# Down projection of a two-layer hybrid encoder: seven products of quarters for a pair of output blocks, with attention buffers in shared memory

## The chip, the cores and the metric

The kernel runs on one core of a Trainium2 chip. The metric is the device time of one execution in microseconds (us), the median of several runs. PE is TensorE, DVE VectorE, ACT ScalarE, POOL GpSimd and SP SyncE, which issues most DMAs.

## The reference

One inference step of an encoder with two layers (`DEPTH = 2`), for a prompt of 512 positions and a sample of 32 positions that share all weights; model width 1024, hidden width 4096. Each layer is

```
x = x + W_out(concat[A(h), B(h), C(h)]),  h = rms_norm(x, g_mix)
hf = rms_norm(x, g_ffn)
x = x + jnp.square(jax.nn.relu(hf @ w_up)) @ w_down
```

A, B and C are a spatial gate, a short convolution and a sparse attention whose keys an indexer picks (top k). The outputs are x after the second layer and the new cache rows. The change concerns the last line, the product with `w_down` (4096 x 1024).

## The kernel before, in words

x stays in SBUF feature-major: 8 blocks of 128 features by 544 positions, as two tiles, one for each half of the positions (`xs[0]` with 256 and `xs[1]` with 288 columns). A float32 product is made of three float32r products: each operand is split into a part `hi` (a cast on ACT) and a part `lo` (a subtraction on DVE), and hi·hi, lo·hi and hi·lo are summed in PSUM (`mm3`, L225 to L227).

Weights come in through `load_w` (L205): SP issues a DMA of 512 KB into one of two `raw` buffers, ACT casts its 1024 columns to `hi` (L216), DVE (for a few loads POOL) makes `lo` (L217), and both go into a ring of 3072 columns, so three such loads are on hand ahead of PE.

The feed-forward of a layer is cut into four chunks c of 1024 hidden features. A chunk has an **up phase**, 8 blocks f of 128 features, each 8 k-blocks x 3 matmuls for each half (L225 to L227, the moving operand `h0hi` to `h1lo`), after which ACT takes relu (L957), DVE squares (L958) and `split` writes `hi` and `lo` of the activations (L221 and L222: `a0hi` to `a1lo`). Its **down phase** is 8 output blocks m, each 24 matmuls for each half with the activations as moving operand; `add_to_x` (L908) on DVE adds the sum in PSUM to x. So a down phase is 8 x 2 x 24 = 384 matmuls, half of them 256 and half 288 columns wide.

At the end of layer 0 the last three output blocks are taken together, all of the first half and then all of the second, so that the norm of the first half (`norm`, L252 to L258: a matmul with ones, rsqrt with a Newton step, then 8 blocks scaled and split) lies beside the second half's matmuls. At the end of layer 1 the transposed results (`results`, L273 to L277) of one half of the positions lie in the same way beside the matmuls of the other.

The order on each engine is fixed when the program is built: a scheduler takes what is ready, by a priority that favours copies out of PSUM (`EVAC`) and then weight loads (`PREP`). At run time every engine works through its list in that order.

Of the kernel before, what the change touches and what calls it, by code (L numbers as in the profile page):

```python
# [7 lines left out]
F32 = mybir.dt.float32  # L8
F32R = mybir.dt.float32r
# [6 lines left out]
D = 1024  # L16
# [4 lines left out]
HALF = (256, 288)  # L21
EPS = 1e-6
# [3 lines left out]
# column groups of w_in  # L26
# [12 lines left out]
class Shift:  # L39
    """Shifts the scheduling priority of what is traced inside."""  # L40
# [12 lines left out]
def kernel(  # L53
# [13 lines left out]
    rawp = ctx.enter_context(tc.tile_pool(name="rawp", bufs=2))  # L67
# [48 lines left out]
    busy = keep([128, 512], "qrs")  # L116
# [5 lines left out]
    spare = keep([128, 2, D], "a1hi"), keep([128, D], "a0hi")  # L122
    xin += [spare[0][:, 0], spare[0][:, 1], spare[1]]
    # per-feature vectors as columns: g_mix, g_ffn, conv_w, state_conv
# [20 lines left out]
    xs = [keep([128, 8, n], f"x{i}") for i, n in enumerate(HALF)]  # L145
# [11 lines left out]
    junk = keep([128, 2, D], "a0lo")  # L157
# [61 lines left out]

    def split(hi, lo, src):  # L220
# [43 lines left out]
    def results(b, g, tag):  # L264
        """A block's output, half of its features, back to token-major."""
# [15 lines left out]
    def prepare(l):  # L281
# [42 lines left out]
    def search_constants():  # L324
# [3 lines left out]
        # for the threshold search: prefix sums, the copies' total, steps  # L328
# [15 lines left out]
    for l in range(depth):  # L344
# [20 lines left out]
        def tok_gemm(b, pieces, n, aside=True):  # L365
            """Token-major product of a block; aside: the sample's rows by themselves, in float32."""
# [678 lines left out]
```

## Time and profile before

| | |
|---|---|
| median of 3 runs (lowest to highest) | 1400.22 us (1398.63 to 1400.79) |
| span of the profiled execution | 1403.4 us |
| busy: PE, DVE, ACT, POOL | 1353.1, 840.0, 615.9, 115.3 us |
| mean granted TensorE clock | 0.982 of full speed |

The profile is of one execution on the chip. A row of a group names line, engine, operation, output and inputs and shapes; a row of a timeline starts with the start and the length in us; in square brackets stands the idle time of that engine just before and what ended it. The length of a matmul is longer than its distance to the next, since matmuls are pipelined. Times below are of this execution.

### The profile page before, as it was taken

The page shows a single profiled execution, that of the slowest core. Times are in us where ns is not written, and L with a number is a line of the kernel's source. Part 1 is how long each engine was busy: PE and PEld are TensorE (multiplying, and loading weights), DVE is VectorE, ACT ScalarE, POOL GpSimd, SP SyncE. Part 2 cuts the span into 40 slices and gives each one's busy share as a digit, 9 for nine tenths or more (in the row PEclk, how much of TensorE's full clock was granted, in tenths as well). Part 3 has the DMA queues.
Part 4 walks back from the last instruction along what each step waited for, and adds up shares of the span by engine and source line. Part 5 has one row for each costly group of instructions (what it writes and reads, how often), then busy time and mean ns, then how long its engine had stood idle before and what let it go on. Part 6 is the DMA issues. An engine that isn't in the chain of part 4 may idle for free. (4 is left out here: it accounts for less than half of the span.)

```text
span 1403.4 us, 25751 instructions
## 1 busy us (share of the span) xinstructions
PE 1353.1 (96%) x10430; PEld 1265.8 (90%) x10430; DVE 840.0 (60%) x2103; ACT 615.9 (44%) x1212; POOL 115.3 (8%) x125
## 2 busy tenths in 40 slices
PE   7998999998999999999989899999899999999998
PEld 5877886898999999999987789779799999999998
DVE  6999987468434334334489999865853343443442
ACT  5746996335314224223246489842542231331321
POOL 4414200010000000000042120000200000000000
PEclk8999999999999999999988999999999999999999
DMA  7124221323233332333212222222233332233322
GB/s 185 33 71 106 68 64 48 94 68 89 81 88 91 91 84 84 89 91 91 64 49 62 58 81 77 76 61 61 61 95 88 91 91 86 82 90 91 91 81 74
DMA packets 183566, 113.00 MB, mean 81 GB/s; under 512 B 7028, under 2 KB 180616, under 8 KB 183448
## 3 DMA queue, kind: packets, MB, share of 16 engines
q1 hardware_dynamic: 180808, 106.35, 26.2%
q0 software_dynamic: 2640, 5.01, 1.8%
q8 instruction: 82, 1.34, 0.4%
q14 instruction: 36, 0.29, 0.1%
HBM read 106.67 MB, written 4.67 MB: 79 GB/s over the span
## 5 line engine op out<-in xcount | busy, mean ns | idle before, releaser
L216 ACT CAST hi<-raw 128x1024 fp32r<-128x1024 f32 (+1 forms) x188 | 194.1, 1032 | 404.6 <-PE psm L226 389.1
L217 DVE TENSOR_TENSOR lo<-raw,hi 128x1024 fp32r<-128x1024 f32 (+1 forms) x163 | 197.5, 1212 | 174.9 <-ACT hi L216 174.2
L908 DVE TENSOR_TENSOR x<-x,psm 128x256 f32<-128x256 f32 (+1 forms) x192 | 83.7, 437 | 232.4 <-PE psm L227 232.0
L226 PE MATMUL psm<-h1lo,hi 128*128 128x288 f32 x640 | 190.4, 298 | 0.9 <-DVE h1lo L222 0.9
L227 PE MATMUL psm<-a1hi,lo 128*128 128x288 f32 x640 | 190.0, 297 | 0.0
L226 PE MATMUL psm<-a1lo,hi 128*128 128x288 f32 x640 | 189.9, 297 | 0.0
L225 PE MATMUL psm<-a1hi,hi 128*128 128x288 f32 x640 | 189.8, 297 | 0.0
L225 PE MATMUL psm<-h1hi,hi 128*128 128x288 f32 x640 | 188.7, 296 | 1.1 <-ACT h1hi L221 1.1
L227 PE MATMUL psm<-h1hi,lo 128*128 128x288 f32 x640 | 189.1, 296 | 0.0
L226 PE MATMUL psm<-h0lo,hi 128*128 128x256 f32 x640 | 181.9, 285 | 6.2 <-DVE h0lo L222 6.2
L225 PE MATMUL psm<-a0hi,hi 128*128 128x256 f32 x640 | 183.0, 286 | 0.0
L226 PE MATMUL psm<-a0lo,hi 128*128 128x256 f32 x640 | 182.0, 284 | 0.0
L227 PE MATMUL psm<-a0hi,lo 128*128 128x256 f32 x640 | 182.0, 284 | 0.0
L225 PE MATMUL psm<-h0hi,hi 128*128 128x256 f32 x640 | 181.4, 284 | 0.0
L227 PE MATMUL psm<-h0hi,lo 128*128 128x256 f32 x640 | 180.0, 282 | 0.0
L226 PEld LDWEIGHTS psm<-h0lo,hi 128*128 128x128 f32 x640 | 120.4, 188 | 8.6 <-DVE h0lo L222 7.1
L225 PEld LDWEIGHTS psm<-h1hi,hi 128*128 128x128 f32 x640 | 120.1, 188 | 2.7 <-ACT h1hi L221 1.5
L225 PEld LDWEIGHTS psm<-a0hi,hi 128*128 128x128 f32 x640 | 121.6, 190 | 0.5 <-issue 0.5
L226 PEld LDWEIGHTS psm<-h1lo,hi 128*128 128x128 f32 x640 | 120.3, 188 | 1.8 <-DVE h1lo L222 1.3
L226 PEld LDWEIGHTS psm<-a0lo,hi 128*128 128x128 f32 x640 | 121.2, 189 | 0.6 <-issue 0.5
L225 PEld LDWEIGHTS psm<-h0hi,hi 128*128 128x128 f32 x640 | 120.6, 189 | 1.2 <-issue 0.9
L227 PEld LDWEIGHTS psm<-a0hi,lo 128*128 128x128 f32 x640 | 121.6, 190 | 0.0
(318 smaller groups left out, 2841.1 us busy)
## 6 DMA issues: line engine op xcount, KB each, us to landing
raw<-in_w_up_dram SPq DMA_DIRECT2D x64, 512.0 KB, 4.1
raw<-in_w_down_dram SPq DMA_DIRECT2D x64, 512.0 KB, 3.9
raw<-in_w_in_dram SPq DMA_DIRECT2D x36, 512.0 KB, 3.9
raw<-in_w_out_dram SPq DMA_DIRECT2D x8, 512.0 KB, 3.8
raw<-in_w_out_dram SPq DMA_DIRECT2D x32, 128.0 KB, 3.0
raw<-in_w_in_dram SPq DMA_DIRECT2D x8, 296.0 KB, 6.1
q<-in_cache_k_dram SPq DMA_DIRECT2D x4, 512.0 KB, 4.3
h1lo<-in_cache_v_dram SPq DMA_DIRECT2D x2, 1024.0 KB, 7.1
```

The source lines that it names most:

```text
L216: nc.scalar.copy(hi, raw)
L217: (eng or nc.vector).tensor_tensor(lo, raw, hi.bitcast(F32), op=ALU.subtract)
L225: nc.tensor.matmul(out, lhsT=st[0], rhs=mv[0], start=first, stop=False)
L226: nc.tensor.matmul(out, lhsT=st[0], rhs=mv[1], start=False, stop=False)
L227: nc.tensor.matmul(out, lhsT=st[1], rhs=mv[0], start=False, stop=last)
L908: nc.vector.tensor_tensor(xs[h][:, m, :], xs[h][:, m, :], p[:, :HALF[h]], op=ALU.add)
```

## The change

For a chunk, the weights of a **pair** of output blocks (m1, m2) are four quarters: L11 and L21 are the first 512 hidden features for m1 and for m2, L12 and L22 the other 512. The activations are four quarters too: R11 and R12 the first four f-blocks for positions 0 to 271 (A) and 272 to 543 (B), R21 and R22 the other four. Sums of quarters are made on DVE: T1 = R12 - R11, T2 = R22 - T1, T3 = R22 - R12, T4 = R21 - T2 once a chunk, and S1 = L21 + L22, S2 = S1 - L11, L12 - S2 and L11 - L21 for each pair. Seven products of 4 k-blocks x 3 matmuls, 272 columns wide, take the place of the eight that four quarter products of each side need. They are summed in three PSUM tiles (tags l, d, o), and after each of the seven DVE adds a tile to one quarter of x. The weights are split after the sums, in pieces of 512 columns (`split_w`), so the ring holds six pieces. x is one tile, `raw` has three buffers, the scratch memory of POOL's DMAs is set to 8192 bytes, and the activations R11, R21, R22 and T1 lie in `ahi`/`alo`; T2, T3 and T4 lie in six buffers `e0` to `e5` that the attention uses for keys, values, scores and queries. Both norms at the end of layer 0, and all five blocks of results of the last 512 features of layer 1, now come after the last product.

```diff
-    rawp = ctx.enter_context(tc.tile_pool(name="rawp", bufs=2))
+    rawp = ctx.enter_context(tc.tile_pool(name="rawp", bufs=3))
...
+    def split_w(src, a, c):
+        with prep:
+            if ring[2] + a * c > RING:
+                ring[2] = 0
+            hi, lo = (t[:, ring[2]:ring[2] + a * c].rearrange("p (k c) -> p k c", k=a) for t in ring[:2])
+            ring[2] += a * c
+            nc.scalar.copy(hi, src)
+            nc.vector.tensor_tensor(lo, src, hi.bitcast(F32), op=ALU.subtract)
+        return [(hi[:, k], lo[:, k]) for k in range(a)]
+    def sum_w(a, b, op):
+        with prep:
+            t = T(512, "tt").rearrange("p (k c) -> p k c", k=4)
+            nc.vector.tensor_tensor(t, a, b, op=op)
+        return t
...
+        kTp = keep([128, 2, NT], "e0")
+        Vp = keep([128, 4, 256], "e1")
+        works = keep([128, SK], "e2")
+        qTs = keep([128, 2, 2, 2, 128], "e3")
+        mixed = keep([128, 1024], "e4")
+        work3, qrs = mixed[:, :512], mixed[:, 512:].rearrange("p (u c) -> p u c", u=2)
+        kiTq = keep([128, NT + 256], "e5", F32R)
+        kiTp = kiTq[:, :NT]
...
-            act = [(keep([128, 8, n], f"a{h}hi", F32R), keep([128, 8, n], f"a{h}lo", F32R)) for h, n in enumerate(HALF)]
-            for fs in ((0, 1, 2), (3,), (4,), (5,), (6,), (7,)) if c == 0 else [(f,) for f in range(8)]:
...
+                for f in fs:
+                    k = f % 4
+                    if f < 4:
+                        put(R11, k, hidden[f][:, :EVEN])
+                        continue
+                    r1, r2 = hidden.pop(k), hidden.pop(f)
+                    t12, t34 = T(NT + NS, "pt"), T(NT + NS, "pt")
+                    A, B = slice(0, EVEN), slice(EVEN, 2 * EVEN)
+                    sub = lambda o, a, b: nc.vector.tensor_tensor(o, a, b, op=ALU.subtract)
+                    sub(t12[:, A], r1[:, B], r1[:, A])
+                    split(*(t[:, R21:R22 + 1, k, :] for t in first4), r2.rearrange("p (a n) -> p a n", a=2))
+                    put(T1, k, t12[:, A])
+                    sub(t12[:, B], r2[:, B], t12[:, A])
+                    put(T2, k, t12[:, B])
+                    sub(t34[:, A], r2[:, B], r1[:, B])
+                    sub(t34[:, B], r2[:, A], t12[:, B])
+                    put(T3, k, t34[:, A])
+                    put(T4, k, t34[:, B])
...
-            last, end = c == 3 and l + 1 < depth, c == 3 and l + 1 == depth
-            for ms in ((0,), (1,), (2,), (3,), (4,), (5, 6, 7)) if c == 3 else [(m,) for m in range(8)]:
-                ws = [load_w(w_down[l, c * 1024:c * 1024 + 1024, m * 128:m * 128 + 128], 8, 128) for m in ms]
-                for h in (1, 0) if end else (0, 1):
-                    for m, w in zip(ms, ws):
-                        p = fm_gemm(h, act, w)
-                        add_to_x(h, m, p)
...
+            def product(p, w, o, first=True):
+                for k in range(4):
+                    st, mv = w[k], [t[:, k, :] for t in parts_of[o]]
+                    for a, b in ((0, 0), (0, 1), (1, 0)):
+                        nc.tensor.matmul(p[:, :EVEN], lhsT=st[a], rhs=mv[b], start=first and (k, a, b) == (0, 0, 0),
+                                         stop=(k, a) == (3, 1), skip_group_check=True)
+            def quarters(i):
+                rows = lambda q: w_down[l, c * 1024 + q * 512:c * 1024 + q * 512 + 512, i * 256:i * 256 + 256]
+                ra, rb = load_raw(rows(0), 4, 256), load_raw(rows(1), 4, 256)
+                l11, l21, l12, l22 = ra[:, :, :128], ra[:, :, 128:], rb[:, :, :128], rb[:, :, 128:]
+                part = lambda v: split_w(v, 4, 128)
+                yield part(l11)
+                s1 = sum_w(l21, l22, ALU.add)
+                yield part(s1)
+                s2 = sum_w(s1, l11, ALU.subtract)
+                yield part(s2)
+                yield part(sum_w(l12, s2, ALU.subtract))
+                yield part(l12)
+                yield part(sum_w(l11, l21, ALU.subtract))
+                yield part(l22)
...
+            for i in range(4):
+                m1, m2 = 2 * i, 2 * i + 1
+                w = quarters(i)
+                pa, pb, pd = psum("l"), psum("o"), psum("d")
+                product(pa, next(w), R11)
+                add(m1, 0, pa)
+                product(pd, next(w), T1)
+                add(m2, 1, pd)
+                finish()
+                product(pa, next(w), T2, first=False)
+                add(m1, 1, pa)
+                product(pd, next(w), R22, first=False)
+                add(m1, 1, pd)
+                product(pb, next(w), R21)
+                add(m1, 0, pb)
+                product(pa, next(w), T3, first=False)
+                add(m2, 1, pa)
+                def end_pair(pa=pa, w=w, m1=m1, m2=m2):
+                    product(pa, next(w), T4, first=False)
+                    add(m2, 0, pa)
+                    squares_of(m1)
+                late.append(end_pair)
+                if end and i == 2:
+                    for b, tag in enumerate("mxmxm"):
                         results(b, 0, tag)
+            finish()
+            if last:
+                for h in range(2):
+                    hn.append(norm(h, o_gm + 8 * (l + 1)))
+            if end:
+                for b, tag in enumerate("mxmxm"):
+                    results(b, 1, tag)
...
-    nc = _bacc.Bacc("TRN2", target_bir_lowering=False, num_devices=1)
+    nc = _bacc.Bacc("TRN2", target_bir_lowering=False, num_devices=1, dynamic_dma_scratch_size=8192)
```

How the instructions move on the engines is seen at three places.

DVE within a down phase (chunk 1 of layer 0), the preparation of weights (`lo`) and the additions to x. Before:

```order
764 L217 TENSOR_TENSOR lo<-raw_4755,hi 128x1024
765 L908 TENSOR_TENSOR x_8_105<-x_8_105,psm_4647 128x256
766 L908 TENSOR_TENSOR x_9_106<-x_9_106,psm_4673 128x288
767 L217 TENSOR_TENSOR lo<-raw_4811,hi 128x1024
768 L908 TENSOR_TENSOR x_8_105<-x_8_105,psm_4703 128x256
769 L908 TENSOR_TENSOR x_9_106<-x_9_106,psm_4729 128x288
```

Now, from the second addition of a pair's fourth product on (L244 are sums of weights, the tiles `t_` hold them, `ps` are PSUM tiles):

```order
951 L1030 TENSOR_TENSOR x_104<-x_104,psd_5755 128x272
952 L244 TENSOR_TENSOR t_5976<-raw_5876 128x512
953 L238 TENSOR_TENSOR lo<-t_5927,hi 128x512
954 L1030 TENSOR_TENSOR x_104<-x_104,pso_5754 128x272
955 L238 TENSOR_TENSOR lo<-t_5944,hi 128x512
956 L1030 TENSOR_TENSOR x_104<-x_104,psl_5753 128x272
957 L238 TENSOR_TENSOR lo<-raw_5878,hi 128x512
958 L1030 TENSOR_TENSOR x_104<-x_104,psl_5873 128x272
959 L238 TENSOR_TENSOR lo<-t_5976,hi 128x512
960 L244 TENSOR_TENSOR t_6015<-raw_5996,raw_5998 128x512
961 L1030 TENSOR_TENSOR x_104<-x_104,psd_5875 128x272
962 L238 TENSOR_TENSOR lo<-raw_5996,hi 128x512
```

Two splits of 1024 columns and four additions to a pair of blocks have become seven splits of 512, four sums of 512 and seven additions of 272 columns.

DVE at the turn from the up to the down phase of the same chunk, with the last block of activations (L958 and L1007 are the squares, L222 and L249 the `lo` of activations, L1016 the differences). Before:

```order
757 L958 TENSOR_TENSOR t_4552<-t_4552 128x256
758 L222 TENSOR_TENSOR a0lo_4072<-t_4552,a0hi_4071 128x256
759 L217 TENSOR_TENSOR lo<-raw_4699,hi 128x1024
760 L958 TENSOR_TENSOR t_4582<-t_4582 128x288
761 L908 TENSOR_TENSOR x_8_105<-x_8_105,psm_4591 128x256
762 L222 TENSOR_TENSOR a1lo_4074<-t_4582,a1hi_4073 128x288
763 L908 TENSOR_TENSOR x_9_106<-x_9_106,psm_4617 128x288
764 L217 TENSOR_TENSOR lo<-raw_4755,hi 128x1024
```

Now (`ahi` and `alo` of two 272-column pieces are R21 and R22, `e_931` is T2 and `e_933` T3):

```order
919 L1007 TENSOR_TENSOR t_5577<-t_5577 128x288
920 L244 TENSOR_TENSOR t_5856<-raw_5756 128x512
921 L1030 TENSOR_TENSOR x_104<-x_104,psl_5648 128x272
922 L238 TENSOR_TENSOR lo<-raw_5756,hi 128x512
923 L1030 TENSOR_TENSOR x_104<-x_104,psd_5650 128x272
924 L249 TENSOR_TENSOR alo_5097<-t_5577,ahi_5096 128x2x272
925 L238 TENSOR_TENSOR lo<-t_5775,hi 128x512
926 L1016 TENSOR_TENSOR t_5632<-t_5577,t_5632 128x272
927 L1016 TENSOR_TENSOR t_5633<-t_5577,t_5516 128x272
928 L1016 TENSOR_TENSOR t_5633<-t_5577,t_5632 128x272
929 L249 TENSOR_TENSOR e_932_5099<-t_5632,e_931_5098 128x272
930 L249 TENSOR_TENSOR e_934_5101<-t_5633,e_933_5100 128x272
```

The differences and splits of the last block, and with them T2, stand behind the additions of the first two products.

PE at the end of layer 0. Before, from the last down matmuls into the products of layer 1's indexer (`h0hi` is the first half's norm):

```order
4799 L225 MATMUL psm_7992<-a1hi_6965,hi 128x288
4800 L226 MATMUL psm_7992<-a1lo_6966,hi 128x288
4801 L227 MATMUL psm_7992<-a1hi_6965,lo 128x288
4802 L225 MATMUL psm_8093<-hi,h0hi_7900 128x296
4803 L226 MATMUL psm_8093<-lo,h0hi_7900 128x296
4804 L227 MATMUL psm_8093<-hi,h0lo_7901 128x296
```

Now (`psx` is the sum of squares for the norms, L279):

```order
4603 L1037 MATMUL psl_8083<-e_1103_7166,hi 128x272
4604 L1037 MATMUL psl_8083<-e_1104_7167,hi 128x272
4605 L1037 MATMUL psl_8083<-e_1103_7166,lo 128x272
4606 L279 MATMUL psx_8243<-work_1161_7873,ones 128x256
4607 L279 MATMUL psx_8286<-work_1163_7877,ones 128x288
4608 L252 MATMUL psm_8365<-hi,h0hi_8252 128x296
4609 L253 MATMUL psm_8365<-lo,h0hi_8252 128x296
4610 L252 MATMUL psm_8407<-hi,h0hi_8252 128x296
```

The sums for both norms stand between the last product and the indexer, where before the indexer followed the last product at once.

## Rows read from the trace of the kernel before

**Rows 1.** The page: span, and busy time with share and instructions of each engine.
```profile
span 1403.4 us, 25751 instructions
PE 1353.1 (96%) x10430; PEld 1265.8 (90%) x10430; DVE 840.0 (60%) x2103; ACT 615.9 (44%) x1212; POOL 115.3 (8%) x125
```

**Rows 2.** Windows: length; busy us (count) of PE, PEld, DVE, ACT, POOL; PEclk; DMA; GB/s.
```profile
369.60:418.20 48.60, 48.60 (x386) 48.60 (x385) 17.09 (x25) 9.14 (x10) 0.00 (x0) 1.00 0.30 87
418.20:466.60 48.40, 48.40 (x386) 48.40 (x385) 22.23 (x39) 19.23 (x38) 0.00 (x0) 1.00 0.31 88
338.00:700.00 362.00, 362.00 (x2871) 362.00 (x2870) 152.63 (x255) 110.41 (x193) 0.00 (x0) 1.00 0.31 88
709.90:738.10 28.20, 22.68 (x140) 21.04 (x142) 22.56 (x61) 11.93 (x32) 12.71 (x15) 0.84 0.14 40
```

**Rows 3.** Timeline, down projection in layer 0: start, length, engine, line, operation.
```profile
411.99 0.29 PE L227 MATMUL psm<-a1hi,lo 128*128 128x288 f32 x1
412.12 0.28 PE L225 MATMUL psm<-a0hi,hi 128*128 128x256 f32 x1
412.24 0.29 PE L226 MATMUL psm<-a0lo,hi 128*128 128x256 f32 x1
412.32 0.45 DVE L908 TENSOR_TENSOR x<-x,psm 128x288 f32<-128x288 f32 x1 [2.78 <-PE psm L227]
```

**Rows 4.** Groups by shape, whole span: busy us, mean ns, idle before, releaser.
```profile
L217 DVE TENSOR_TENSOR lo<-raw,hi 128x1024 fp32r<-128x1024 f32 x158 | 193.5, 1224 | 172.2 <-ACT hi L216 171.6 <-DMA raw<-in_w_out_dram 0.5
L908 DVE TENSOR_TENSOR x<-x,psm 128x288 f32<-128x288 f32 x96 | 43.5, 453 | 166.7 <-PE psm L227 166.7
L908 DVE TENSOR_TENSOR x<-x,psm 128x256 f32<-128x256 f32 x96 | 40.2, 420 | 65.8 <-PE psm L227 65.3
L222 DVE TENSOR_TENSOR a0lo<-t,a0hi 128x256 fp32r<-128x256 f32 x72 | 30.6, 425 | 29.2 <-ACT a0hi L221 29.2
L216 ACT CAST hi<-raw 128x592 fp32r<-128x592 f32 x8 | 5.5, 685 | 4.3 <-DMA raw<-in_w_in_dram 3.0 <-PE psm L226 1.3
```

**Rows 5.** Timeline of DVE in an up projection, instructions that follow without a wait.
```profile
425.47 1.23 DVE L217 TENSOR_TENSOR lo<-raw,hi 128x1024 fp32r<-128x1024 f32 x1 [2.44 <-ACT hi L216]
426.61 0.45 DVE L958 TENSOR_TENSOR t<-t 128x288 f32<-128x288 f32 x1
427.56 0.46 DVE L222 TENSOR_TENSOR a1lo<-t,a1hi 128x288 fp32r<-128x288 f32 x1 [0.50 <-ACT a1hi L221]
427.94 0.42 DVE L958 TENSOR_TENSOR t<-t 128x256 f32<-128x256 f32 x1
```

**Rows 6.** Groups of DVE in the down projection at 369.6 to 418.2.
```profile
L217 DVE TENSOR_TENSOR lo<-raw,hi 128x1024 fp32r<-128x1024 f32 x8 | 9.8, 1226 | 5.8 <-ACT hi L216 5.8
```

**Rows 7.** Timeline at the end of layer 0.
```profile
713.30 0.41 PE L227 MATMUL psm<-hi,h0lo 128*128 128x296 f32 x1 [0.90 <-DVE h0lo L222]
716.03 1.33 PE L252 MATMUL psx<-work,ones 128*128 128x288 f32 x2 [2.19 <-DVE work L242]
721.60 0.45 PE L226 MATMUL psm<-lo,h0hi 128*128 128x296 f32 x1
721.84 0.45 PE L227 MATMUL psm<-hi,h0lo 128*128 128x296 f32 x1
...
722.40 0.30 PE L227 MATMUL psm<-hi,h0lo 128*128 128x296 f32 x1
...
726.44 1.19 DVE L222 TENSOR_TENSOR h1lo<-t,h1hi 128x288 fp32r<-128x288 f32 x3
```

**Rows 8.** DMA issues of the page: KB each, median us to landing.
```profile
raw<-in_w_down_dram SPq DMA_DIRECT2D x64, 512.0 KB, 3.9
out_dram<-t SPq DMA_DIRECT2D x8, 256.0 KB, 2.1
```

**Rows 9.** Timeline at the end of the program.
```profile
1397.70 0.28 PE L227 MATMUL psm<-a0hi,lo 128*128 128x256 f32 x1
1399.52 0.82 SPq L277 DMA_DIRECT2D out_dram<-t  x2
```

More of the change, by code (lines that the diff above doesn't have):

```diff
@@ L21 @@
 HALF = (256, 288)
+EVEN = (NT + NS) // 2
+QTR = 4 * EVEN
 EPS = 1e-6
@@ L121 @@
     xin = [Q([128, D]), Q([128, D])]
-    spare = keep([128, 2, D], "a1hi"), keep([128, D], "a0hi")
-    xin += [spare[0][:, 0], spare[0][:, 1], spare[1]]
+    spare = keep([128, 4 * QTR], "ahi")
+    xin += [spare[:, i * D:i * D + D] for i in range(3)]
     NV = 8 * depth * 2 + 6 * depth + 4 * depth
@@ L218, in load_w, with load_raw @@
         return [(hi[:, k], lo[:, k], raw[:, k]) for k in range(a)]
+    def load_raw(src, a, c):
+        with prep:
+            raw = rawp.tile([128, a, c], F32, tag="raw", name=nm("raw"))
+            nc.sync.dma_start(raw, src.rearrange("(k p) c -> p k c", p=128))
+        return raw
+    def split_w(src, a, c):
[8 more added lines that the diff above has]
+    def sum_w(a, b, op):
+        with prep:
+            t = T(512, "tt").rearrange("p (k c) -> p k c", k=4)
+            nc.vector.tensor_tensor(t, a, b, op=op)
+        return t
     def split(hi, lo, src):
@@ L570 @@
                     nc.vector.tensor_copy(wsel[:, :, a, :], pt[:, :64].rearrange("p (g t) -> p g t", g=2))
-                work = keep([128, SK], "works")
+                work = works
                 for c0, cn in ((0, 512), (512, 512), (1024, 32)):
@@ L944, with put @@
         hn = []
+        R11, R21, R22, T1, T2, T3, T4 = range(7)
         for c in range(4):
-            act = [(keep([128, 8, n], f"a{h}hi", F32R), keep([128, 8, n], f"a{h}lo", F32R)) for h, n in enumerate(HALF)]
-            for fs in ((0, 1, 2), (3,), (4,), (5,), (6,), (7,)) if c == 0 else [(f,) for f in range(8)]:
+            last, end = c == 3 and l + 1 < depth, c == 3 and l + 1 == depth
+            first4 = [keep([128, 4, 4, EVEN], tag, F32R) for tag in ("ahi", "alo")]
+            rest = [[keep([128, 4, EVEN], f"e{3 * i + j}", F32R) for i in range(2)] for j in range(3)]
+            parts_of = [[t[:, o] for t in first4] for o in range(4)] + rest
+            def put(o, k, src):
+                split(parts_of[o][0][:, k, :], parts_of[o][1][:, k, :], src)
+            hidden = {}
+            order = (0, 4, 1, 5, 2, 6, 3, 7)
+            groups = [order[:3]] + [(f,) for f in order[3:]] if c == 0 else [(f,) for f in order]
+            for fs in groups:
                 ws = []
@@ L950 @@
                     c0 = (c * 8 + f) * 128
-                    ws.append(load_w(w_up[l, :, c0:c0 + 128], 8, 128, nc.gpsimd if c == 0 and f < 3 else None))
+                    ws.append(load_w(w_up[l, :, c0:c0 + 128], 8, 128, nc.gpsimd if c == 0 and f in order[:3] else None))
+                    hidden[f] = T(NT + NS, "g")
                 for h, n in enumerate(HALF):
@@ L968, with finish, squares_of @@
+            late = []
+            def finish():
+                while late:
+                    late.pop()()
+            def squares_of(m0):
+                if last:
+                    for m in (m0, m0 + 1):
+                        for h in range(2):
                             add_square(h, m)
@@ L970 @@
                                 heat(h, m)
-                    if last and len(ms) == 3:
-                        hn.append(norm(h, o_gm + 8 * (l + 1)))
-                    if end and len(ms) == 3:
-                        for b, tag in ((0, "l"), (1, "x")) if h == 0 else ((2, "l"), (3, "x"), (4, "o")):
-                            results(b, 1, tag)
-                if end and ms == (4,):
-                    for b, tag in enumerate("lxold"):
-                        results(b, 0, tag)
+            for i in range(4):
[22 more added lines that the diff above has]
+                    for b, tag in enumerate("mxmxm"):
+                        results(b, 0, tag)
+            finish()
+            if last:
+                for h in range(2):
+                    hn.append(norm(h, o_gm + 8 * (l + 1)))
+            if end:
+                for b, tag in enumerate("mxmxm"):
+                    results(b, 1, tag)
         hs = hn
```

30 lines of the change are left out of this document (15 added, 15 removed).

## The prediction

> **What bounds the kernel now.** I read the page first: the span is 1403.4 us and PE is busy for 1353.1 of it, no other engine for more than 60% [rows 1]. The profiled execution is 3.2 us longer than the median of 1400.22, so I make the sum on 1403.4 and take 3.2 off at the end. Then the windows, because a mean over stages says nothing of one: in a down phase and in an up phase of the feed-forward PE is busy every microsecond, DVE 17.09 of 48.60 and 22.23 of 48.40, and the clock is at its upper level, 2.4 GHz [rows 2]. The reader is to see there that the feed-forward is paced by matmuls alone: 2871 of them fill 362.00 us, 126.1 ns each. Third, the timeline, for what one matmul costs: the next starts 0.13 us after one of 288 columns and 0.12 us after one of 256 [rows 3], though each is 0.28 or 0.29 us long. Distance counts, not length; it grows with the columns, and 272 lie in the middle, so I take the mean of 126.1 ns for them. Last, the groups by shape and DVE's timeline, for the new work.
>
> **The matmuls.** Eight down phases have 384 each, 3072. The change has 7 products x 12 x 4 pairs x 8 = 2688. 384 fewer at 126.1 ns: **-48.4 us**, all of it on the path. A pair goes from 96 x 0.1261 = 12.11 us to 84 x 0.1261 = 10.59, a product takes 1.51.
>
> **DVE in the down phase.** A pair needs 7 `lo` and 4 sums of 512 columns and 7 additions of 272. No row has these shapes. By length, 512 lie between 425 ns (256 columns) and 1224 ns (1024): 425 + 256/768 x 799 = 691; 272 between 420 and 453: 437 [rows 4]. But neighbours overlap: after the 1.23 us split the next instruction starts 1.14 us later, after one of 0.46 us 0.38 later [rows 5], so DVE is held some 0.085 us less: 0.605 and 0.35. A pair costs 11 x 0.605 + 7 x 0.35 = 9.1 us, against 10.59 of PE: 86%, where today it is 17.09 / 48.60 = 35% [rows 2]. ACT has 7 casts of under 0.685 us [rows 4], under 4.8 us. So the work lies beside the matmuls, but the cover is thin, and two things can lift it. First, the order of PE is fixed, and a product that goes on in a PSUM tile (S2·T2 on L11·R11) waits for the addition that reads it; one other product, 1.51 us, stands between, and an addition starts about 0.33 us after the last matmul of its sum [rows 3], 0.35 later it is done: 0.8 us to spare, one piece of preparation. Second, three `raw` buffers serve pairs that take two, so a pair's second load starts only when the sum L11 - L21 of the pair before is made, and takes 3.9 us [rows 8]; in the new order four products' additions stand between, some 4.5 us, and the sum that needs it would hold up DVE by little. I take 0.2 us a pair, 32 x 0.2 = **+6 us**; ends 0 and 0.7 a pair (+22), the latter a missed hand-over of one 512-column piece each time.
>
> **DVE in the up phase.** For two blocks f, four differences, one split of 544 and five of 272 columns replace four splits: 9 x 0.35 + 0.65 - 4 x 0.35 = 2.4 us, so a phase goes from 22.2 to about 32 us of 48.4 [rows 2]. Covered, nothing. In the first chunk of a layer it falls beside the norms: +0.5 each, **+1 us**.
>
> **The turn from up to down.** Today the last block's split is needed 24 matmuls later. Now T2, T3 and R21/R22 of the last k-block stand in DVE's list behind the additions of the first two products. From the last up matmul on: square, sum and addition end at about 2.2 us, `lo` and the second addition (its product ends at 3.0) at 3.7, then split of 544, `lo` and three differences, 0.65 + 0.6 + 1.05 = 2.3, so T2 is whole at about 6.4. PE has 45 matmuls, 5.7 us, that do not need it, and then a few that need only its `hi`. It waits for some 0.4: 8 x 0.4 = **+3 us**. Ends 0 and 2.5 (the whole DVE run uncovered), +20.
>
> **The end of layer 0.** Today the first half's norm runs beside 72 matmuls, and still the stretch from there to the end of the indexer's five blocks takes 28.20 us with PE busy 22.68 and a clock of 0.84 [rows 2]: PE waits for 0.90 and 2.19 us, and from the second wait on the distance of its matmuls is 0.24 us, the level of 1.2 GHz, for about 6 us, until 0.13 returns [rows 7]. Now nothing runs beside either norm: addition, squares, their sums, matmul, rsqrt, three steps, scaling and cast follow each other, ten steps of about 0.45 us, 4.5 us. Then 48 matmuls of 0.135, paced by 16 DVE steps of about 0.36 (three take 1.19 us [rows 7]), 6.5; then the ropes of two blocks before the second half is scaled, 3; then 72 matmuls, 9.7; and 3 us for a slow clock as today: 26.7, and 0.7 for the last product of the pair, which waits for the addition of the one before. That is a microsecond less than today, with a longer list of waits; I take **+2 us**, ends -3 and +12 (the low level for the whole stretch, 120 x 0.105).
>
> **The last pair and the tail.** The sums of weights take buffers from which results are being written out; a store needs 2.1 us to land [rows 8] and stands between: 1 to 2 us. At the end five result blocks remain after the last matmul instead of two; today the last store is issued 1.8 us after it [rows 9], now one more pair of transposes and copy, 1.1 us. Together **+3 us**, ends +1 and +6. What the norms of layer 0 share with the attention buffers is free by then: the attention of a layer ends before its output projection. The smaller scratch memory concerns POOL, 8% busy [rows 1], and nothing on the path.
>
> **Sum.** 1403.4 - 48.4 + 6 + 1 + 3 + 2 + 3 = 1370.0 us; less 3.2 it is **1367 us**.
>
> **The rivals.** *DVE sets the pace of the down phases.* If each instruction holds DVE for its whole length, a pair costs 11 x 0.691 + 7 x 0.437 = 10.7 us, more than PE's 10.59, and the first sum and cast of a pair (0.6 us) come on top: 11.3 a pair, a gain of 0.8 x 32 = 26 and with 12 us for the ends 1386 us. Against it stands the overlap in rows 5. [...] Chance 0.15.
>
> *Every `lo` waits for its cast: slower.* Today a `lo` in a down phase finds DVE idle for 5.8 / 8 = 0.73 us until ACT has cast [rows 6]. With seven a pair on a DVE that works through its list in order, 9.1 + 7 x 0.73 = 14.2 us, 2.1 more than 12.11: 32 x 2.1 = +67, with 12 for the ends 1479 us. It decides from (12.11 - 9.1)/7 = 0.43 us a `lo` on. Against it: a ring of six pieces lets a cast start five products ahead, and the order of DVE puts other work between a sum and its `lo`. Chance 0.06.
>
> *The ends lose their cover.* 2.5 us at each turn and 10 at the end of layer 0: 1367 + 17 + 8 = 1392 us. For it speaks that DVE is behind after an up phase; against it that PE's order puts other products ahead of T2. Chance 0.09.
>
> *It doesn't save what it counts.* If 272 columns go at the distance of 288, 0.1325, the products cost 2688 x 0.1325 = 356 us against 387, a gain of 31 in place of 48: 1384 us. Rows 3 show a distance that grows with columns. Chance 0.04.
>
> **How the numbers follow.** The forecast has 0.66 and spans 1350 (all of the 48 us, the ends as low as they go) to 1380. The range reaches to the two rivals at 1384 and 1386 and part of the way to 1392: 1350 to 1390. Only the second rival is slower; a measurement here tells 0.2%, 2.8 us, from no change. Faster 0.92, same 0.02, slower 0.06.
>
> **What would show it.** Right: in a window of a down phase PE busy all through, 336 matmuls in 42 to 44 us, DVE about 36 of it, distances of 0.126 us; at each turn a wait of under 1 us on `e3` or `e0`. Wrong: PE waiting for `lo` or for `x` in every pair (the first two rivals), DVE over 95% in that window, waits of 2 us at the turns, or the clock at 1.2 GHz for much longer than 6 us after layer 0.

## The result, and the profile after

The changed kernel takes **1362.27 us** (median of 5 runs, 1359.95 to 1367.17) against 1398.63 for the kernel before in the same comparison: ratio 0.9742, 95% interval 0.9718 to 0.9766, a gain of 36 us where 33 were forecast. The profiled execution is the longest of the five (1367.17; span 1365.4), so where its stages are compared below, a second profile of the same kernel stands beside it.

The page of after, the lines that answer to [rows 1]:

```profile
span 1365.4 us, 25930 instructions
PE 1308.2 (96%) x10046; PEld 1220.7 (89%) x10046; DVE 1079.1 (79%) x2679; ACT 709.8 (52%) x1436; POOL 111.9 (8%) x125
```

PE has 384 matmuls fewer and is as full as before; DVE has gone from 60 to 79%. The windows of after, columns as in [rows 2]: 27 products of the down phase of chunk 0 in layer 0, the whole down phase of chunk 1, the up phase of chunk 2, the end of layer 0.

```profile
368.01:409.05 41.04, 41.04 (x327) 40.96 (x326) 34.78 (x68) 18.18 (x30) 0.00 (x0) 1.00 0.32 95
459.27:503.05 43.78, 43.78 (x347) 43.57 (x346) 36.18 (x69) 18.18 (x30) 0.00 (x0) 1.00 0.34 98
503.18:550.51 47.33, 47.33 (x376) 47.33 (x375) 34.00 (x67) 22.16 (x46) 0.00 (x0) 1.00 0.29 88
684.50:712.00 27.50, 21.82 (x122) 20.51 (x121) 20.53 (x61) 9.57 (x27) 6.79 (x11) 0.81 0.13 39
```

The reader is to see PE busy in every microsecond of a down phase, with DVE at 36.18 of 43.78 (the window holds the 336 matmuls of the phase and a few of the next up phase). 27 products are 324 matmuls in 41.04 us, 126.7 ns each; the distance that was taken is 126.1. A chunk begins 91.25 us after the one before it (368.01, 459.27, 550.51, 641.77) where it was 97.0, so a chunk is worth 5.75 us and eight of them 46. That is 2.4 us less than the 48.4 of the prediction: all 720 matmuls of a chunk go at 126.7 ns, where the 768 of before went at 126.3. DVE's timeline in that phase, the lines that answer to [rows 5]:

```profile
472.37 0.68 DVE L238 TENSOR_TENSOR lo<-raw,hi 128x512 fp32r<-128x512 f32 x1
472.98 0.69 DVE L244 TENSOR_TENSOR t<-t,raw 128x512 f32<-128x512 f32 x1
473.58 0.43 DVE L1030 TENSOR_TENSOR x<-x,psl 128x272 f32<-128x272 f32 x1
473.93 0.69 DVE L238 TENSOR_TENSOR lo<-t,hi 128x512 fp32r<-128x512 f32 x1
```

Start to start it is 0.60 after 512 columns and 0.35 after 272, the two prices of the prediction (0.605, 0.35), and the lengths are 0.69 and 0.43 (0.691, 0.437). The groups of these shapes over the span, with the idle time that stands in front of them:

```profile
L238 DVE TENSOR_TENSOR lo<-t,hi 128x512 fp32r<-128x512 f32 x128 | 88.2, 689 | 14.1 <-ACT hi L237 11.1
L238 DVE TENSOR_TENSOR lo<-raw,hi 128x512 fp32r<-128x512 f32 x96 | 66.1, 689 | 9.0 <-ACT hi L237 5.0
L1037 PE MATMUL psl<-e,hi 128*128 128x272 f32 x768 | 151.9, 292 | 1.1 <-DVE x L1030 1.1
```

A `lo` waits for its cast for 16.1 us over 224 of them, 0.07 us each, where [rows 6] had 0.73. The last row holds the only wait of PE inside the seven products of the whole program: 1.1 us, in the last pair of layer 0. PE's timeline of the end of layer 0, rows with a wait in front alone (compare [rows 7]), and the wait that came new behind it:

```profile
684.03 0.48 PE L1037 MATMUL psl<-e,hi 128*128 128x272 f32 x2 [1.07 <-DVE x L1030]
687.21 0.70 PE L279 MATMUL psx<-work,ones 128*128 128x256 f32 x2 [1.44 <-DVE work L269]
688.90 0.75 PE L279 MATMUL psx<-work,ones 128*128 128x288 f32 x2 [0.99 <-DVE t L157]
690.78 0.62 PE L252 MATMUL psm<-hi,h0hi 128*128 128x296 f32 x1 [1.12 <-ACT h0hi L248]
702.47 0.41 PE L252 MATMUL psm<-hi,h1hi 128*128 128x296 f32 x1 [2.12 <-ACT h1hi L248]
...
724.74 0.37 PE L106 MATMUL psl<-idr,ks 128*128 128x128 f32 x1 [4.62 <-ACT t L582]
```

The span is 38.0 us shorter than that of before. Eight chunks give -46.0. From the last product of layer 0 (685.49) to the last matmul of the indexer (715.56) it is 30.1 us, before 27.6: +2.5. The last down phase and the tail together lose 1. The start, up to the first product of layer 0, is 1.6 shorter (368.0 for 369.6), which says nothing: in the ten profiles of the changed kernel and its variants it takes from 361.7 to 368.0 us. What is left is +6.0 between 715.56 and the first product of layer 1 (1038.62): 323.1 us where it was 317.0. The prediction had 0.5 us there (DVE beside the norms in the first chunk), and the experiments go after the rest.

### The profile page after: what moved, and what is told of

Read it like the earlier page. It is cut to its first block, busy times and chain, and to the rows that moved or that the text cites. A ratio compares the mean times of both kernels' runs of the same rounds, so it can differ in the third digit from the quotient of the medians.

```text
span 1365.4 us, 25930 instructions
## 1 busy us (share of the span) xinstructions
PE 1308.2 (96%) x10046; PEld 1220.7 (89%) x10046; DVE 1079.1 (79%) x2679; ACT 709.8 (52%) x1436; POOL 111.9 (8%) x125
## 4 chain that ended last, share of the span: by engine, by line
PE 82%; DVE 11%; issue 3%; ACT 2%; DMA 2%; POOL 0%; SPq 0%; ACTq 0%; DVEq 0%; POOLq 0%
PE psm L253 16%; PE psm L252 16%; PE psm L254 15%; PE psl L1037 14%; PE psd L1037 7%; PE pso L1037 4%; PE psl L722 2%; PE psx L106 2%; PE pso L752 1%; DVE t L285 1%; PE psd L106 1%; DVE m L441 1%; DVE work L442 1%; DMA ahi<-in_x_prompt_dram 1%; DVE lo L221 1%
## 5 line engine op out<-in xcount | busy, mean ns | idle before, releaser
L220 ACT CAST hi<-raw 128x1024 fp32r<-128x1024 f32 (+1 forms) x124 | 127.0, 1025 | 139.1 <-PE psm L253 65.2
L221 DVE TENSOR_TENSOR lo<-raw,hi 128x1024 fp32r<-128x1024 f32 (+1 forms) x99 | 120.4, 1217 | 79.9 <-ACT hi L220 79.5
L1037 PE MATMUL psl<-e,hi 128*128 128x272 f32 x768 | 151.9, 292 | 1.1 <-DVE x L1030 1.1
L237 ACT CAST hi<-t 128x512 fp32r<-128x512 f32 x128 | 79.7, 622 | 90.1 <-PE psl L1037 30.1
L1037 PEld LDWEIGHTS psl<-e,hi 128*128 128x128 f32 x768 | 121.1, 188 | 2.8 <-ACT hi L220 1.3
L254 PEld LDWEIGHTS psm<-h0hi,lo 128*128 128x128 f32 x640 | 123.2, 193 | 0.3 <-issue 0.2
L254 PEld LDWEIGHTS psm<-h1hi,lo 128*128 128x128 f32 x640 | 120.6, 188 | 0.9 <-issue 0.9
L1037 PE MATMUL psl<-e,lo 128*128 128x272 f32 x384 | 111.1, 289 | 0.0
L238 DVE TENSOR_TENSOR lo<-t,hi 128x512 fp32r<-128x512 f32 x128 | 88.2, 689 | 14.1 <-ACT hi L237 11.1
L237 ACT CAST hi<-raw 128x512 fp32r<-128x512 f32 x96 | 59.7, 622 | 72.2 <-PE psl L1037 36.5
```

Of the source, the lines that this page charges most:

```text
L220: nc.scalar.copy(hi, raw)
L221: (eng or nc.vector).tensor_tensor(lo, raw, hi.bitcast(F32), op=ALU.subtract)
L237: nc.scalar.copy(hi, src)
L238: nc.vector.tensor_tensor(lo, src, hi.bitcast(F32), op=ALU.subtract)
L254: nc.tensor.matmul(out, lhsT=st[1], rhs=mv[0], start=False, stop=last)
L1037: nc.tensor.matmul(p[:, :EVEN], lhsT=st[a], rhs=mv[b], start=first and (k, a, b) == (0, 0, 0), stop=(k, a) == (3, 1), skip_group_check=True)
```

## The experiments

The kernel before ran beside each of them on the same chip; ratios are to it. The order of the parts: the third buffer and the shared memory, DVE's cover, the order of the products, POOL.

**A second profile of the changed kernel** (no edit).

> The changed kernel as it is, for a second profile of it, beside the others on one chip. Theory (the 4.6 us wait behind the indexer's `t` at the start of layer 1 belongs to the kernel): 1360 to 1366 us, the wait is there again between 4 and 5 us, and from the last product of layer 0 to the first of layer 1 it is 352 to 354 us again (353.1). Rival (that stretch was long in that one execution, whose 1367.17 was the longest of five): under 350 us.

Measured: 1359.72 us, ratio 0.9714 (0.9687 to 0.9741). Both theories hold in part. The wait is there again with 4.6 us, so it belongs to the kernel; the stretch from the last product to layer 1's first is 683.23 to 1031.26, 348.0 us, so 5 of its 353.1 were that one execution's. The same 60 us of layer 1 as a window, of this profile and then of the first one:

```profile
778.00:838.00 60.00, 54.25 (x444) 46.75 (x442) 58.70 (x206) 48.83 (x87) 12.34 (x13) 1.00 0.31 88
```
```profile
778.00:838.00 60.00, 55.01 (x419) 47.05 (x420) 55.25 (x196) 44.80 (x79) 13.01 (x14) 0.91 0.29 82
```

The granted clock of PE is 1.00 in the one and 0.91 in the other, where it is 0.50 from 803 to 813, and there 419 matmuls were done in the time of 444. Against before (344.6 us) the stretch loses 3.4, not 8.5: 1.3 up to the indexer's end, 2.1 behind it.

**The buffers alone**: the old feed-forward in the new memory.

```diff
-        R11, R21, R22, T1, T2, T3, T4 = range(7)
...
+            both = keep([128, 4 * QTR], "ahi", F32R), keep([128, 4 * QTR], "alo", F32R)
+            act = [tuple(t[:, 8 * 256 * h:8 * (256 * h + n)].rearrange("p (k n) -> p k n", k=8) for t in both) for h, n in enumerate(HALF)]
...
```

> The changed kernel with the feed-forward of before (eight products of halves), so with its shared attention buffers and its third raw buffer alone. Theory 1 (the third raw buffer bunches the weight splits that POOL makes at the start of layer 1, and DVE's subtractions of two SBUF operands stand still beside them): the new waits in layer 1's attention, about 6 us, come with the buffers, 1398.6 + 4 to 6 = 1403 to 1405 us, a PE wait of over 4 us behind an indexer `t`, POOL splits back to back there. Rival (the new end of layer 0 shifts that work): the attention is as before, 1396 to 1399 us, no such wait. In both the feed-forward goes as before, 97.0 us a chunk.

Measured: 1399.61 us, ratio 1.0002 (0.9987 to 1.0017). The rival has the time, theory 1 only a part of the rows: POOL's two splits stand back to back here too (729.12, 4.69 us), but no wait is over 4 us; PE waits 1.62 us for one of the splits and later 2.16. And the trace shows no time lost by it: from the last product of layer 0 to the first of layer 1 it is 343.7 us, where before took 344.6. Shared attention buffers, a third raw buffer and the smaller scratch memory come to nothing as a whole; a chunk of the feed-forward takes 96.75 us (364.11 to 460.86) for 97.0.

**Two raw buffers in place of three.**

```diff
-    rawp = ctx.enter_context(tc.tile_pool(name="rawp", bufs=3))
+    rawp = ctx.enter_context(tc.tile_pool(name="rawp", bufs=2))
```

> The changed kernel with two raw buffers in place of three. Theory 1 (third buffer bunches POOL's splits): the 4.6 us wait at the start of layer 1 goes or halves, and since l22 of a pair is split some 2.8 us after the pair's first matmul and a load takes 3.9 us, the next pair's first piece is ready by 8.5 us of its 10.6: no waits in the down phases, 1357 to 1361 us. Rival (the price that the prediction put on a late hand-over, 0.7 us a pair): 1362 + 22 = 1384 us, PE waits for `hi` or `lo` at the beginning of each pair, and PE busy under 95% in a down phase.

Measured: 1385.29 us, ratio 0.9902 (0.9882 to 0.9922), 26 us over the changed kernel (1359.72 in the run above). The rival has the time, within 1.3 us, though PE is still busy for 96%: a down phase takes 46.2 us (554.21 to 600.41) in place of 43.8, 0.6 a pair on the mean, and a chunk 94.74 in place of 91.25. It isn't a wait at each pair's beginning alone: of the 1.96 us in which PE stands idle in this phase, 1.24 come at its end, in front of the first matmuls of the up phase (598.81), whose weights come late as well. The window of that phase, and the rows of ACT's and DVE's timeline that say what is late:

```profile
554.21:600.41 46.20, 44.24 (x339) 42.76 (x337) 36.89 (x71) 17.00 (x29) 0.00 (x0) 1.00 0.26 81
```
```profile
571.23 1.34 ACT L237 CAST hi<-raw 128x512 fp32r<-128x512 f32 x2 [2.17 <-PE psl L1037]
```
```profile
576.12 0.69 DVE L244 TENSOR_TENSOR t<-raw,raw 128x512 f32<-128x512 f32 x1 [1.19 <-DMA raw<-in_w_down_dram]
```

The last casts from a pair's raw parts wait 2.17 us for a place in the ring, that is for PE, and begin 8 us behind the pair's first matmul (563.35), where theory 1 had the split of l22 done after 2.8; the next pair's load begins only then, and its first sum stands still for it. So the third buffer carries most of what the seven products gain. What theory 1 said of POOL came half true: the splits at the start of layer 1 stand apart (725.29 and 728.19) and the wait of 4.62 us is 2.55, but the stretch to layer 1's first product is 347.9 us, as long as in the second profile (348.0).

**DVE's cover.** Sums made twice, into the same tile.

```diff
+            for _ in range(1 + again):
+                nc.vector.tensor_tensor(t, a, b, op=op)
...
-                s1 = sum_w(l21, l22, ALU.add)
+                s1 = sum_w(l21, l22, ALU.add, 1)
...
-                yield part(sum_w(l11, l21, ALU.subtract))
+                yield part(sum_w(l11, l21, ALU.subtract, 1))
```

> The changed kernel with two of a pair's four sums of weights made twice: two more 512-column additions a pair on DVE, 64 in all. Theory (an instruction holds DVE for its distance, 0.605 us): 36.18 / 4 = 9.05 + 1.21 = 10.26 us a pair, still under PE's 10.6: 1362 to 1366 us, DVE about 41 of 43.8 us in a down phase, PE busy nearly all of it. Rival (DVE held for the whole length, so that the cover was already used up): 11 x 0.689 + 7 x 0.437 + 2 x 0.689 = 12.0 us a pair, 1.4 more than PE: 1362 + 45 = 1407 us.

Measured: 1370.12 us, ratio 0.9791 (0.9772 to 0.9811). An undisturbed down phase grows from 43.79 to 43.99 us with DVE busy for 38.21 (about 41 were forecast):

```profile
456.81:500.80 43.99, 43.99 (x348) 43.57 (x346) 38.21 (x74) 17.72 (x30) 0.00 (x0) 1.00 0.32 98
```

So the theory holds in the phases, and the rival, 45 us, is out, but the time is 4 us over the theory's range. The 10 us in all over the changed kernel lie mostly outside undisturbed phases: the last phase of layer 0 takes 48.1 in place of 43.7, with a wait of 4.08 us behind an addition to x, the last of layer 1 47.75 in place of 45.69. The wait of 4.08 us is no lack of room on DVE. In front of that addition stand three sums of squares of 288 columns, which last 4.75 us beside three splits on POOL; the part on POOL below takes this up:

```profile
679.79 4.64 POOL L221 TENSOR_TENSOR lo<-raw,hi 128x592 fp32r<-128x592 f32 x3 [363.75 <-DVE work L270]
```
```profile
680.00 4.75 DVE L270 TENSOR_TENSOR work<-work,t 128x288 f32<-128x288 f32 x3
```

What the other 2 us of layer 1's last phase wait for was not tried.

The other two sums of a pair made twice too (same edit on S2 and L12 - S2):

> The changed kernel with all four sums of weights of a pair made twice: four more 512-column additions a pair, 128 in all. Theory (distance decides): DVE needs 9.05 + 4 x 0.605 = 11.47 us a pair, 0.85 more than PE's 10.6: 32 x 0.85 = +27, 1389 us, and DVE is busy all through a down phase. Rival (whole length): 13.4 us a pair, 1451 us. If the ends pay as well, as they did with two more sums, 7 us come on top of either.

Measured: 1381.06 us, ratio 0.9864 (0.9835 to 0.9893).

```profile
456.26:501.15 44.89, 44.61 (x347) 43.74 (x346) 41.94 (x82) 17.74 (x31) 0.00 (x0) 1.00 0.29 85
501.15:548.59 47.44, 47.44 (x377) 47.44 (x376) 36.43 (x72) 21.73 (x45) 0.00 (x0) 1.00 0.33 99
```

Whole length is out again (1451). By distance a phase needs 45.9 us of DVE, and it takes 44.9; part of the work (72 instructions in place of 67 in the up phase) has moved to the up phase, where DVE has 11 us to spare. So DVE's room is not that of a down phase alone: the pieces split ahead carry a little of it over. The forecast of 1389 was 8 too high, and 15 with the 7 us that it allowed for the ends: from one chunk to the next the undisturbed phases pay 1.1 us (92.33 for 91.25) where 3.4 were forecast, and the larger part of the 21 us over the changed kernel lies outside them.

**A shorter lead of the weights**: four places in the ring, not six.

```diff
-            if ring[2] + a * c > RING:
+            if ring[2] + a * c > 2048:
```

> The changed kernel with the pieces of the down phases kept to four places of the ring of split weights, not six: a piece can be split three products (4.5 us) ahead instead of five. Theory (cast and `lo` take 0.62 + 0.69 us, so that three are enough): 1359 to 1364 us, PE busy all through. Rival (the lead is what keeps `lo` from waiting for its cast, 0.73 us each as before): from 0.43 us a `lo` on DVE is late; 2.1 us a pair at 0.73, up to 1427 us, and DVE idle in front of `lo` behind ACT in each pair.

Measured: 1359.74 us, ratio 0.9709 (0.9693 to 0.9725), the changed kernel's own. A cast three products ahead is early enough here; it is the load, not the split, that needs the lead (1385.29 us with two raw buffers).

**T4 at once.**

```diff
-                late.append(end_pair)
+                end_pair()
```

> The changed kernel with the product of T4 written right behind that of T3, not behind the first two products of the next pair. Theory (each pair then pays the hand-over of its PSUM tile, 1.07 us as the last pair of layer 0 does): 24 pairs have a pair behind them in their phase, +26 us, 1388 us. Rival (the scheduler that lays out PE's order puts the next pair's first product, which has a PSUM tile of its own, into the gap): 1361 to 1366 us.

Measured: 1367.08 us, ratio 0.9761 (0.9735 to 0.9788), 7 over the changed kernel. A down phase takes 44.14 us with PE busy all through, against 43.79: the scheduler does put the next pair's first product into the gap, and the hand-over costs 0.09 us a pair, not 1.07. Nearer to the rival, which forecast 1366 at most; the rest is the last phase (47.91 for 45.69) and layer 1's attention.

**POOL's splits on DVE.** Of the 4.62 us wait the rows before it say more. DVE's and POOL's timelines in the first profile of after:

```profile
716.36 5.32 DVE L554 TENSOR_TENSOR ks<-t,ks 128x32 fp32r<-128x32 f32 x2
```
```profile
716.80 4.71 POOL L221 TENSOR_TENSOR lo<-raw,hi 128x1024 fp32r<-128x1024 f32 x2
```

Two subtractions of 32 columns last 5.32 us and end with POOL's two splits of weights, which begin one behind the other. The edit, in `load_w`:

```diff
-            (eng or nc.vector).tensor_tensor(lo, raw, hi.bitcast(F32), op=ALU.subtract)
+            nc.vector.tensor_tensor(lo, raw, hi.bitcast(F32), op=ALU.subtract)
```

> The changed kernel with all 25 weight splits that POOL makes moved to DVE (1.14 us each there, 2.4 on POOL). Theory (while POOL makes a split, a DVE instruction with two SBUF operands stands still, so each costs DVE up to 2.4 us now): the 4.6 us wait at the start of layer 1 goes, the instructions of 2.5 us on DVE are gone, 1354 to 1360 us. Rival (in the attention DVE is busy for 28 to 30 of 30 us, and 28 us more work come onto it): 1366 to 1375 us, more waits of PE on DVE there.

Measured: 1355.62 us, ratio 0.9685 (0.9671 to 0.9700). The theory holds. DVE's timeline of the same place (the first row is one of the splits that came over from POOL: DVE had none between 700 and 726 us):

```profile
710.45 1.23 DVE L221 TENSOR_TENSOR lo<-raw,hi 128x1024 fp32r<-128x1024 f32 x1 [0.44 <-ACT hi L220]
712.06 0.29 DVE L554 TENSOR_TENSOR ks<-t,ks 128x32 fp32r<-128x32 f32 x2
```

The pair of subtractions takes 0.29. DVE's busy time over the span falls from 1079.1 to 1069.9 us although 25 splits came onto it. PE's idle time falls by more than the gain of 4.1 us, from 58.0 us of the second profile to 42.3. But its busy time rises for the same matmuls, from 1300.0 to 1311.9 us, at a granted clock of 0.979 in place of 0.986 (0.978 to 0.980 in the four runs here, 0.980 to 0.986 in the four of the second profile).

> The kernel before with POOL's 25 weight splits on DVE, nothing else. Theory (a split on POOL costs DVE up to 2.4 us wherever it stands, against 1.14 on DVE itself): it gains as much as the changed kernel did by the same edit, 4 us or more: 1392 to 1396 us. Rival (it costs only where two stand back to back and PE has no other work, as in the changed kernel at the start of layer 1): 1398 to 1401 us.

The same line in the kernel before: 1390.55 us, ratio 0.9934 (0.9915 to 0.9953), 9.8 us faster. So the loss is not the change's; both kernels had it, and with POOL's splits on DVE in both the change is worth 35 us (1390.55 to 1355.62), about what it is worth with them. The page of this run and the group of the splits on DVE:

```profile
PE 1349.4 (97%) x10428; PEld 1256.3 (91%) x10430; DVE 824.1 (59%) x2128; ACT 613.5 (44%) x1208; POOL 56.6 (4%) x100
```
```profile
L217 DVE TENSOR_TENSOR lo<-raw,hi 128x1024 fp32r<-128x1024 f32 x180 | 220.3, 1224 | 177.0 <-ACT hi L216 176.6
```

That group has grown by 26.8 us against [rows 4], yet DVE's busy time went down from 840.0 [rows 1] to 824.1: some 43 us of it had been standing still. PE's idle time falls here from 50.3 to 37.4 us, and its busy time, unlike in the changed kernel, doesn't rise (1353.1 to 1349.4).

**Another last pair.** In the last pair of a layer R21 comes second, T4 has a PSUM tile of its own, R22 is last, and the first half's norm is started before it.

```diff
+                product(pb, part(l12), R21)
...
+                pc = psum("o")
+                product(pc, part(l22), T4)
+                add(m2, 0, pc)
+                product(pa, part(sum_w(l11, l21, ALU.subtract)), T3, first=False)
+                add(m2, 0, pa)
...
+                    hn.append(norm(0, o_gm + 8 * (l + 1)))
+                product(pd, part(sum_w(l12, s2, ALU.subtract)), R22, first=False)
```

> The changed kernel (1359.7 us beside these runs) with the other last pair of each layer alone, POOL's splits left where they are. Theory (the hand-over wait and the uncovered norm): 2 to 4 us less, 1356 to 1358 us. If all that the two edits gave together beyond POOL's splits came from here: 7.5 less, 1352. Rival (what it frees at the end of layer 0 is waited for again behind POOL's two splits): 1359 to 1361 us, the 4.6 us wait longer.

Alone: 1357.60 us, ratio 0.9690 (0.9670 to 0.9711), 2 less than the changed kernel and at the edge of what can be told. The last down phase of layer 0 is 1.3 us shorter, but from its start to the indexer's end it is 72.5 us as before it (72.6): layer 0's end gains nothing, and the 4.5 us wait behind POOL is there again, as the rival said, though the time lies in the theory's range. The gain is the tail's, 51.8 us from the last phase's start in place of 53.0.

> The changed kernel with POOL's splits on DVE (1355.6 us by itself) and another last pair in each layer: R21 second, T2 before T1, the product of T4 in a PSUM tile of its own, R22 last, and the first half's norm started ahead of R22. Theory (the 1.07 us hand-over and the uncovered norm cost what they show): the wait goes and a product of 1.51 us covers part of the norm, some 2.5 us at the end of layer 0 and up to 1 at the end of the program: 1351.5 to 1354 us. Rival (DVE's list there is what lasts, with one addition more): 1355 to 1357 us.

With POOL's splits on DVE: **1348.09 us, ratio 0.9628 (0.9605 to 0.9651)**, the fastest version, 3.7% under the kernel before and faster than the theory said. Against POOL's edit alone, from the start of layer 0's last down phase to the indexer's end it is 3.2 us shorter (70.0 for 73.2), the tail 1.0, and the attention behind it 3.3. The windows of the first and the third of these, POOL's edit alone above, both edits below:

```profile
639.01:712.20 73.19, 67.05 (x476) 64.84 (x474) 63.86 (x155) 36.41 (x81) 6.94 (x11) 0.93 0.24 69
712.20:1027.58 315.38, 304.98 (x2334) 263.48 (x2334) 256.59 (x780) 190.60 (x400) 7.25 (x14) 0.98 0.24 70
```
```profile
638.72:708.67 69.95, 63.85 (x476) 62.42 (x474) 64.22 (x156) 36.72 (x81) 7.59 (x12) 0.98 0.24 72
708.67:1020.79 312.12, 302.03 (x2334) 261.37 (x2334) 256.40 (x778) 193.05 (x402) 6.71 (x13) 0.98 0.24 70
```

So the theory has the direction and not the reason. The hand-over wait is gone (0.93 us with POOL's edit alone), but over layer 0's end PE is idle for 6.1 us in both (73.19 - 67.05, 69.95 - 63.85), and behind it for 10.4 and 10.1. Nearly all of the difference in these two windows is PE's busy time for the same number of matmuls, 3.2 and 2.95 us, with a granted clock of 0.93 against 0.98 in the first. With the other last pair alone that stretch has 0.93 too. A wait of 3.8 us on `q` behind the indexer is gone, but waits of 2.1 and 1.1 us have come. Why the clock is higher with both edits stays open.

## Why the prediction was right, and where its terms were off

**The matmuls: right.** 384 fewer at the distance of their neighbours; 126.7 ns against 126.1, and the rival of 132.5 ns for 272 columns is out.

**DVE in the down phase: right, and the sum too careful.** Distances of 0.605 and 0.35 were forecast and are 0.60 and 0.35; 36 us of DVE in the window were forecast and are 36.18. The term of +6 for late hand-overs was the mis-sized one: PE waits nowhere in the pairs, so it measured 0. Its upper end was 0.7 us a pair: that is near what two raw buffers cost (0.6 on the mean, in part as a wait at the end of the phase). The prediction's doubt, a second load that can only start when a sum of the pair before is made, is a real limit, and it sits one buffer lower than it was put. The rival by full lengths fell twice, with two and with four more sums. The length worked out from [rows 4] agrees, 691 ns for 689; the pace of the engine doesn't follow from it (600 start to start). In the up phase about 32 us of DVE were forecast and 34.00 of 47.33 are found, covered as forecast.

**The turns: mechanism right, +3 too much.** 6.4 us from the last up matmul to a whole T2 were forecast. In the second profile the last up matmul starts at 456.90 and T2's `lo` begins at 462.92, with PE on matmuls that need no part of the last block's T2 until 462.83; it is whole at 463.36, 6.46 us after the last up matmul, as forecast. No turn shows a wait. That T2's `hi` is needed first the prediction had counted. What it missed is PE's order at that place, where matmuls of the next product stand between those of T2:

```profile
462.83 0.37 PE L1037 MATMUL psl<-e,hi 128*128 128x272 f32 x1
463.03 0.30 PE L1037 MATMUL pso<-alo,hi 128*128 128x272 f32 x1
463.17 0.29 PE L1037 MATMUL pso<-ahi,lo 128*128 128x272 f32 x1
463.29 0.29 PE L1037 MATMUL pso<-ahi,hi 128*128 128x272 f32 x1
463.42 0.39 PE L1037 MATMUL psl<-e,hi 128*128 128x272 f32 x1
```

The one that needs the `lo` starts at 463.42, 0.06 us after it is there. The margin is that thin.

**The end of layer 0: the waits right, the number by luck.** +2 forecast, +2.5 and +1.3 in the two profiles. The waits are the ones named: addition, squares, sums, rsqrt, and the second half's norm (2.12 us at 702.47). The levels that the prediction writes as 2.4 and 1.2 GHz are granted clocks of 1.00 and 0.50 in the trace of before: at 1.00 matmuls of 288 columns start 0.13 us apart [rows 3], at 0.50 those of 296 columns 0.2465 (717.65 to 721.84), 1.20 columns a ns. But the 27.6 us of before hold a loss that isn't the norms': an addition on DVE that lasts 2.62 us beside a split on POOL (the last row of this part), with a wait of PE of 2.04 us at 736.77 in its train. With POOL's splits on DVE in both kernels the windows from the last product to the indexer's end, before the change above and after it below, are these:

```profile
700.96:723.90 22.94, 21.03 (x139) 19.89 (x137) 20.46 (x62) 11.44 (x32) 9.13 (x12) 0.93 0.18 49
```
```profile
682.60:712.20 29.60, 24.39 (x141) 22.45 (x139) 23.52 (x70) 12.67 (x34) 6.94 (x11) 0.83 0.09 24
```

That is 6.7 us more, half of it idle time of PE, half its busy time at a lower granted clock (0.83 for 0.93). The old feed-forward in the new memory, where POOL's two splits come behind the indexer's end, takes 23.4 us, 5.5 less than the second profile. So the norms that stand bare cost some 6 us, by one execution of each kernel: inside the range given (-3 to +12) and three times the term.

**The tail**: +3 forecast, +1 found.

**Every `lo` waits for its cast: out** (0.07 us a `lo`, and no loss with the lead cut to four pieces).

**What had too small a term:** that the shared attention buffers cost nothing holds as a total (1.0002). But behind the indexer, up to layer 1's first product, the changed kernel lost 2 to 6 us (319.2 and 323.1 for 317.0). PE's wait of 4.62 us behind DVE and POOL's two splits lies there, and yet it isn't what the change lost: with POOL's splits on DVE in both kernels the same stretch is 313.6 us before and 315.4 after, 1.8 longer, and before lost its time to POOL in front of the indexer's end. Where these 2 us go stays open. What POOL's splits cost, both kernels paid, and the trace of before had it in plain sight, a few microseconds behind [rows 7]: an addition of 288 columns that lasts 2.62 us on DVE, beside a split on POOL that begins at 733.02:

```profile
733.18 2.62 DVE L509 TENSOR_TENSOR t<-t,t 128x288 f32<-128x288 f32 x1
```

The prediction looked at POOL's share (8%) and passed on.

So the forecast was 5 us too high (7 by the second comparison): nine microseconds of waits in the pairs and at the turns that didn't come and 2 of the tail, less the 2.4 of the longer distance and what was lost behind the indexer. Two slips of the working change nothing. The 3.2 us taken off at the end are a span less a time; in the later runs the time of an execution is 1.8 us above its span, which would stand on both sides of the sum. And the first two rivals add 12 us for the ends where the sum has 9: by the sum's terms they come to 1383 and 1476 us.

## What to carry to other kernels

When products are traded for sums on another engine, price that engine by the distance between its instructions (here 0.60 and 0.35 us, for lengths of 0.69 and 0.43), take its room from the stage, and then ask how many buffers the loads need for a pair: with one buffer fewer two thirds of this gain were gone here. An engine with a small share of busy time can still cost: look for instructions of the neighbour that last many times as long as their shape takes elsewhere (here 5.32 us in place of 0.29). Give the last sum of a stage an accumulator of its own, and put a product behind it that the next stage doesn't wait for; here that, with the order that goes with it, took 1.3 us off the last down phase of layer 0 and 1.2 off the end of the program. And before a stretch of before and one of after are compared, ask whether another loss lies in one of them: POOL's splits made the cost of the bare norms look a third of its size.

## What the runs showed of the hardware

A split of 1024 columns on POOL takes 2.43 us (mean of 22 in the first profile of after), and DVE instructions with two SBUF operands beside it stood still until it ended: two subtractions of 32 columns took 5.32 us beside two splits, 0.29 without. One with a tensor and a column of SBUF as operands was held up as well: this TENSOR_SCALAR of 256 columns, which takes 0.35 us in the trace of before (740.46), takes 1.25, to just behind the end of a split (716.29):

```profile
713.89 2.40 POOL L221 TENSOR_TENSOR lo<-raw,hi 128x1024 fp32r<-128x1024 f32 x1 [0.19 <-ACT hi L220]
```
```profile
715.18 1.25 DVE L584 TENSOR_SCALAR work<-t,wi 128x256 f32<-128x256 f32 x1 [1.39 <-ACT t L582]
```

POOL doesn't hold up all of them. During the split that starts at 741.52 (2.50 us) in the first profile of after, products with one operand in PSUM keep their pace (0.42 for 256 columns, as in the mean of the 24 of that shape), and the first instruction with two SBUF operands to start in it is 1.66 long in place of 1.23; POOL's split ends at 744.02, 0.58 after that start. A TENSOR_SCALAR of one column (`ti<-ti,ti`) kept its 0.21 beside the split at 152.71 too.

```profile
741.71 0.48 DVE L434 TENSOR_TENSOR t<-psm,tab 128x128 f32<-128x128 f32 x2
742.12 0.42 DVE L432 TENSOR_TENSOR t<-psm,tab 128x256 f32<-128x256 f32 x1
742.46 0.49 DVE L434 TENSOR_TENSOR t<-psm,tab 128x128 f32<-128x128 f32 x2
742.98 0.43 DVE L432 TENSOR_TENSOR e<-psm,tab 32x256 f32<-32x256 f32 x1
743.44 1.66 DVE L221 TENSOR_TENSOR lo<-raw,hi 128x1024 fp32r<-128x1024 f32 x1
```

For this kernel it means that a split moved to POOL to relieve DVE costs DVE up to 2.4 us in place of 1.2: taking all 25 back gave 9.8 us before the change and 4.1 after it.
